# Two-layer diffusion trunk on one core: the first sub-layer's products issued input tile by input tile

## The chip, the cores and the metric

The kernel runs on one core of a Trainium2 chip, as one launch. The metric is device time in microseconds, the median of several runs. TensorE multiplies matrices from SBUF into PSUM, VectorE and ScalarE do element-wise work (VectorE written DVE, ScalarE ACT, TensorE PE in the rows; PEld is TensorE's weight load), GpSimd (POOL) a little, and SyncE (SP) issues nearly all DMAs.

## The reference

Two layers are applied to 128 context tokens and 256 latent tokens with 1024 features. Each layer is: half SwiGLU FFN, token mixing, half SwiGLU FFN, each with an RMS norm and a shift, scale and gate that come from a conditioning vector. The change concerns the input of the very first FFN:

```python
def _modulation(cond, w, b):
    m = jax.nn.silu(cond) @ w + b
    return jnp.split(m[:, None, :], N_MOD, axis=-1)

def _ada_norm(x, g, shift, scale):
    return _rms(x, g) * (1 + scale) + shift

def _half_ffn(x, shift, scale, gate, g, w1, w3, w2):
    h = _ada_norm(x, g, shift, scale)
    f = (jax.nn.silu(h @ w1) * (h @ w3)) @ w2
    return x + 0.5 * gate * f
```

The FFN has 2816 hidden features, 22 tiles of 128. All is fp32; layer 0 mixes tokens by gated linear attention and a Fourier transform, layer 1 by windowed attention.

## The kernel before, in words

Activations lie with features along the partitions: `x` is 8 input tiles of 128 features by 384 tokens. Each fp32 product is made of three float32r matmuls (`mm3`, L336 to L339): high weights by high input, high weights by low input, low weights by high input. A "unit" of weights is 1 MB; for the first FFN a unit holds the 128 columns of w1 and of w3 that make one hidden feature tile. `load_to` (L305) brings units into three raw buffers, `split_to` (L313) makes of each half a high part (ScalarE cast, L210) and a low part (VectorE subtraction, L211), and `take` (L328) hands a unit out after splitting two units and loading four ahead. There are four buffers for high halves and four for low halves, so two units.

The norm's factor 1/rms is applied behind the products: the products' input is `x * (scale + 1) * g`, split into `hh` and `hl` (`Feed.feed`, L225 to L231), and the shift goes along as two more columns, so that a product has 386 columns. `Norm.finish` (L203) makes the mean of the squares by a matmul, then ln and exp on ScalarE and a Newton step of three instructions on VectorE (`rsqrt`, L175 to L185). `combine` (in `ffn`) multiplies a pair of product tiles by 1/rms (L413), applies silu and the product of the two (L418), and splits the result for the second matrix. A pair of product tiles (w1's and w3's columns of one hidden feature tile; "the pair" below) fills a PSUM tile of two banks; the pool `psp` (L53) has three of them.

The first sub-layer's shift and scale are made at the start (L848 to L886), two input tiles at a time, for q = 0 to 3 (the four "groups"): two 1 MB DMAs of modulation weights, 2 x 16 small matmuls into `mod0_q` (L859; a row of the trace counts their 32 parts), a copy, a transposition by TensorE (L868), bias and scale on VectorE, then `shifts` and `feed` for these two input tiles. Everything runs in the order of the built program on each engine; before, a scheduler chose that order on all engines, by priorities that follow the code, and only the products of input tile 4 were told to follow group 3 (`boot`, `behind`). All other modulation vectors come from dot products on VectorE (`mod_dots`, L149) that run beside the FFN, paced by the number of units taken.

Of the kernel before, what the change touches and what calls it, by code (L numbers as in the profile page):

```python
# [17 lines left out]
P = 128  # L18
# [13 lines left out]
MORE = {1: 2, 2: 3}  # attention block behind which a unit of queries is projected  # L32
TURN = {3: 2, 5: 3}  # and is rotated
LAG = 3  # attention blocks between the scores and the products with the values
# (units of weights taken, feature tiles of the modulations done by then)
MOD_PACE = ((2, 0), (34, 42), (38, 42), (45, 48), (50, 48), (112, 120), (123, 120), (150, 128))
PSC = 0.125  # 64 ** -0.5
# [6 lines left out]
def trunk(ctx, tc, a):  # L44
# [19 lines left out]
    # Activations are kept in runs that share a table set, each behind the load of its set.  # L64
# [29 lines left out]
    # the sub-layer's input (T token columns, then the shifts of the two groups), as two float32r parts  # L94
# [16 lines left out]
    # silu(c) as stationary columns: 0 for the context's condition, 1 for the step's.  # L111
# [29 lines left out]
    def mod_dots():  # L141
        """One feature tile of one vector at a time: a dot product along the free axis for either condition."""
# [18 lines left out]
    def pump():  # L161
        """Keeps the modulations as far ahead as the units of weights taken so far ask for."""
        want = np.interp(at["take"], *zip(*MOD_PACE))
        while done[0] < want:
            next(dots)
            done[0] += 1
# [8 lines left out]
    def rsqrt(mean, n, name):  # L175
        """(mean + eps) ** -0.5 by exp and ln, and one Newton step."""
# [10 lines left out]
    class Norm:  # L187
        """RMS statistics of x, built up as its feature tiles become final."""
# [19 lines left out]
    def split(hi, lo, src):  # L208
        """src = hi + lo, both float32r."""
        act.copy(hi, src)  # L210
        pace["last"] = dve.tensor_tensor(lo, src, f(hi), op=ALU.subtract).ins  # L211

    class Feed(Norm):
        """Input of sub-layer n of layer l: x * (scale + 1) * g, and the shift; 1 / rms is applied behind the products."""
# [18 lines left out]
    class Last(Norm):  # L233
        """The final norm, token group by token group."""
# [78 lines left out]
    def split_to(n):  # L313
        while at["split"] < min(n, len(stream)):
# [5 lines left out]
            for h in range(0, w, 1024):  # L320
                e = min(1024, w - h)
                hi = wts.tile([P, e], F32R, tag="whi", name=f"whi{i}_{h}", bufs=4)
                lo = wts.tile([P, e], F32R, tag="wlo", name=f"wlo{i}_{h}", bufs=4)
# [4 lines left out]
    def take(key):  # L328
        i = at["take"]
        assert stream[i][0] == key, (stream[i][0], key)  # L330
        split_to(i + 2)
        load_to(i + 4)
# [9 lines left out]
    def product(out, u, behind=None):  # L342
        """The sub-layer's input @ 128 columns; behind: a feature tile, and an instruction that its products follow."""
        wh, wl = u
        for k in range(KD):
            i = mm3(out, wh[:, k], wl[:, k], hh[:, k], hl[:, k], k == 0, k == KD - 1)
            if behind and behind[0] == k:
                after(i.ins, behind[1], "modulations before the products")

    def spread(dst, pp, feed):  # L350
        """dst [P, 2, T] = products / rms + the shift's products."""
# [6 lines left out]
    def project(key, feed, dst, name):  # L358
        """dst [P, 2, T] = the sub-layer's input @ a unit of 256 columns."""
# [7 lines left out]
    def project_out(nk, parts, l, v, nxt, name, shared=False, order=None):  # L367
        """x += gate * (parts @ w), 256 output features at a time; feeds the next sub-layer as they become final
        (shared: once the last of them has read the parts, which lie where the next input goes)."""
# [36 lines left out]
    def ffn(l, fi, feed, make_next):  # L406
        name = f"ffn{l}{fi}"
        with tc.tile_pool(name=f"g_{name}", bufs=1) as gp:
# [14 lines left out]
            waiting = []  # L423
# [620 lines left out]
```

## Time and profile before

| | |
|---|---|
| timed runs, median (lowest to highest of 3) | 1467.79 us (1466.99 to 1468.07) |
| profiled execution, first to last instruction (span) | 1466.1 us |
| TensorE, matmuls busy | 1429.0 us, 97% |
| TensorE, weight loads busy | 1382.1 us, 94% |
| VectorE busy | 1087.5 us, 74% |
| ScalarE busy | 600.5 us, 41% |
| DMA moved | 245.27 MB, 167 GB/s in the mean |

The profile is of one execution, whose own time on this page is the span; the timed runs hold some 1.7 us more, which lie around it. Busy shares are means over the whole span; busy times by stretch and the sequence of instructions tell where an engine waits. Matmul ends are modelled, so starts are the firmer numbers. The granted TensorE clock is shown as a share of full speed, 1.00 for 2.4 GHz and 0.50 for 1.2 GHz.

### The profile page before, as it was taken

What the parts mean: (1) busy time and instruction counts of PE and PEld (TensorE: products, weight loads), DVE (VectorE), ACT (ScalarE), POOL (GpSimd) and SP (SyncE); (2) the same over time, 40 slices, a digit from 0 to 9 for tenths busy, and PEclk for the clock granted to TensorE, in tenths of its full rate; (3) what the DMA queues carried; (4) which work ended last, traced back from release to release, by engine and by line L of the source; (5) the groups of instructions that cost most, each with busy time, mean ns of one, the idle gap of its engine ahead of it and who ended that gap; (6) DMA issues with size and microseconds to landing.
All of it is one profiled execution on the core that took longest, in us unless ns stands there. A gap on an engine that the chain in (4) does not pass through costs nothing. (4 is left out here: it accounts for less than half of the span.)

```text
span 1466.1 us, 21497 instructions
## 1 busy us (share of the span) xinstructions
PE 1429.0 (97%) x8508; PEld 1382.1 (94%) x8508; DVE 1087.5 (74%) x1825; ACT 600.5 (41%) x976; POOL 98.6 (7%) x74
## 2 busy tenths in 40 slices
PE   6999999999999999999999999999998999999997
PEld 4999999999889999999999999999975999999996
DVE  3799889869876788888869888885577666666433
ACT  3534434335344444343343433333257444434332
POOL 2000000011102000000100000011120200000001
PEclk8999999999999999999999999999999999999998
DMA  9666656563413456556636655654320233433331
GB/s 393 222 208 201 216 193 232 195 226 117 158 44 137 141 197 199 203 176 230 215 141 215 215 187 187 215 219 154 128 87 1 101 125 138 154 130 110 135 101 43
DMA packets 48516, 245.27 MB, mean 167 GB/s; under 512 B 5376, under 2 KB 9856, under 8 KB 29088
## 3 DMA queue, kind: packets, MB, share of 16 engines
q1 hardware_dynamic: 44560, 240.80, 46.9%
q10 hardware_dynamic: 3856, 3.10, 0.7%
q8 instruction: 67, 1.10, 0.3%
q14 instruction: 33, 0.27, 0.1%
HBM read 241.79 MB, written 2.10 MB: 166 GB/s over the span
## 5 line engine op out<-in xcount | busy, mean ns | idle before, releaser
L210 ACT CAST whi<-raw 128x1024 fp32r<-128x1024 f32 (+1 forms) x317 | 325.6, 1028 | 626.9 <-PE ffn_p L338 307.0
L211 DVE TENSOR_TENSOR wlo<-raw,whi 128x1024 fp32r<-128x1024 f32 (+1 forms) x317 | 380.5, 1201 | 191.5 <-ACT whi L210 189.5
L337 PE MATMUL ffn_p<-hh,whi 128*128 128x386 f32 x1408 | 480.0, 341 | 4.9 <-ACT whi L210 3.0
L338 PE MATMUL ffn_p<-hl,whi 128*128 128x386 f32 x1408 | 478.9, 340 | 3.9 <-DVE hl L229 3.7
L339 PE MATMUL ffn_p<-hh,wlo 128*128 128x386 f32 x1408 | 478.9, 340 | 0.3 <-DVE wlo L211 0.2
L149 DVE SCALAR_TENSOR_TENSOR junk<-modw,cb 128x1024 f32<-128x1024 f32 x256 | 314.1, 1227 | 2.1
L338 PEld LDWEIGHTS ffn_p<-hl,whi 128*128 128x128 f32 x1408 | 267.0, 190 | 7.4 <-DVE hl L229 7.0
L337 PEld LDWEIGHTS ffn_p<-hh,whi 128*128 128x128 f32 x1408 | 266.4, 189 | 6.7 <-ACT whi L210 3.2
L339 PEld LDWEIGHTS ffn_p<-hh,wlo 128*128 128x128 f32 x1408 | 266.5, 189 | 1.5 <-DVE wlo L211 1.3
L337 PE MATMUL ffn_acc<-gh_ffn,whi 128*128 128x384 f32 x704 | 236.6, 336 | 0.0
L338 PE MATMUL ffn_acc<-gl_ffn,whi 128*128 128x384 f32 x704 | 236.6, 336 | 0.0
L339 PE MATMUL ffn_acc<-gh_ffn,wlo 128*128 128x384 f32 x704 | 236.6, 336 | 0.0
L337 PEld LDWEIGHTS ffn_acc<-gh_ffn,whi 128*128 128x128 f32 x704 | 132.4, 188 | 0.0
L339 PEld LDWEIGHTS ffn_acc<-gh_ffn,wlo 128*128 128x128 f32 x704 | 132.4, 188 | 0.0
L338 PEld LDWEIGHTS ffn_acc<-gl_ffn,whi 128*128 128x128 f32 x704 | 132.4, 188 | 0.0
L200 POOL TENSOR_TENSOR ssq_n<-ssq_n,sq_n 128x384 f32<-128x384 f32 x42 | 61.0, 1451 | 946.8 <-ACT sq_n L199 922.4
L413 DVE TENSOR_TENSOR ffn_e<-ffn_p,r_n 128x768 f32<-128x768 f32 x88 | 84.0, 955 | 54.2 <-PE ffn_p L339 54.1
L83 ACT ACTIVATE ffn_e<-ffn_e,ffn_wb 128x128 f32<-128x128 f32 (+1 forms) x176 | 70.4, 449 | 53.3 <-DVE ffn_wb L415 53.1
L211 DVE TENSOR_TENSOR gl_ffn<-ffn_e,gh_ffn 128x384 fp32r<-128x384 f32 x88 | 49.0, 557 | 38.1 <-ACT gh_ffn L210 37.9
L210 ACT CAST gh_ffn<-ffn_e 128x384 fp32r<-128x384 f32 x88 | 45.0, 512 | 62.2 <-DVE ffn_e L418 62.2
L418 DVE SCALAR_TENSOR_TENSOR ffn_e<-ffn_e,ffn_p 128x128 f32<-128x128 f32 (+1 forms) x176 | 65.8, 416 | 0.0
L229 DVE SCALAR_TENSOR_TENSOR hl<-x,mods,hh 128x128 fp32r<-128x128 f32 (+1 forms) x96 | 57.1, 636 | 2.0 <-ACT hh L228 1.2
(245 smaller groups left out, 1224.8 us busy)
## 6 DMA issues: line engine op xcount, KB each, us to landing
raw<-in_w SPq DMA_DIRECT2D x120, 1024.0 KB, 4.8
modw<-in_modw SPq DMA_DIRECT2D x128, 512.0 KB, 3.3
raw<-in_w SPq DMA_DIRECT2D x16, 768.0 KB, 4.9
raw_mod<-in_modw SPq DMA_DIRECT2D x8, 1024.0 KB, 15.3
raw<-in_w_in SPq DMA_DIRECT2D x8, 1024.0 KB, 4.8
raw<-in_w_out SPq DMA_DIRECT2D x8, 1024.0 KB, 4.8
raw<-in_w_og SPq DMA_DIRECT2D x2, 1024.0 KB, 5.0
raw<-in_w_v SPq DMA_DIRECT2D x2, 1024.0 KB, 4.7
```

Source lines behind the costliest of these rows:

```text
L83: i = act.activation(out, in_, func, **kw)
L149: i = dve.scalar_tensor_tensor(junk, raw, 1.0, cb[:, c], op0=ALU.mult, op1=ALU.mult, accum_out=mods[l][v][:, d, c : c + 1])
L200: pool.tensor_tensor(self.ssq, self.ssq, sq, op=ALU.add)
L210: act.copy(hi, src)
L211: pace["last"] = dve.tensor_tensor(lo, src, f(hi), op=ALU.subtract).ins
L229: dve.scalar_tensor_tensor(hl[:, d, t0:t1], x[:, d, t0:t1], sc[:, c : c + 1], f(hh[:, d, t0:t1]), op0=ALU.mult, op1=ALU.subtract)
L337: first = pe.matmul(out, lhsT=wh, rhs=mh, start=start, stop=False)
L338: pe.matmul(out, lhsT=wh, rhs=ml, start=False, stop=False)
L339: pe.matmul(out, lhsT=wl, rhs=mh, start=False, stop=stop)
L413: dve.tensor_tensor(e, pp[:, :, :T], feed.r.unsqueeze(1).broadcast_to([P, 2, T]), op=ALU.mult)
L418: dve.scalar_tensor_tensor(e[:, 1, t0:t1], e[:, 1, t0:t1], pp[:, 1, T + c : T + c + 1], e[:, 0, t0:t1], op0=ALU.add, op1=ALU.mult)
```

## The change

The loop over the groups now issues the products of the first three pairs itself, input tile by input tile: after group q's inputs are fed, pair 0 gets its two new input tiles; from q = 1 on also pair 1 (for q = 1 all four input tiles known by then); from q = 2 on also pair 2. On TensorE the order in this part is the order in which the code is written (`manual_schedule`), where a scheduler chose it before. The loads stand in a loop of their own ahead of it: for q = 0 to 2 a unit of weights behind each group's modulation weights, so the third unit now ahead of group 3's; the modulation weights share five buffers where each of the eight had its own. The third unit is split early, into buffers of the start's own pool. Loads of units 3 to 5 now stand ahead of that of the conditions (`cb`). `ffn` finds three pairs begun, finishes the norm first and combines them ahead of the fourth pair. Comments are dropped throughout; the rest of the code is as before.

```diff
-    def split_to(n):
+    def split_to(n, apart=None):
...
-                hi = wts.tile([P, e], F32R, tag="whi", name=f"whi{i}_{h}", bufs=4)
-                lo = wts.tile([P, e], F32R, tag="wlo", name=f"wlo{i}_{h}", bufs=4)
+                if apart is None:
+                    hi = wts.tile([P, e], F32R, tag="whi", name=f"whi{i}_{h}", bufs=4)
+                    lo = wts.tile([P, e], F32R, tag="wlo", name=f"wlo{i}_{h}", bufs=4)
+                else:
+                    hi = apart.tile([P, e], F32R, name=f"whi{i}_{h}")
+                    lo = apart.tile([P, e], F32R, name=f"wlo{i}_{h}")
...
-    def take(key):
+    def take(key, ahead=True):
...
-        split_to(i + 2)
-        load_to(i + 4)
+        if ahead:
+            split_to(i + 2)
+            load_to(i + 4)
...
-    def product(out, u, behind=None):
+    def product(out, u, ks=range(KD)):
         wh, wl = u
-        for k in range(KD):
-            i = mm3(out, wh[:, k], wl[:, k], hh[:, k], hl[:, k], k == 0, k == KD - 1)
-            if behind and behind[0] == k:
-                after(i.ins, behind[1], "modulations before the products")
+        for k in ks:
+            mm3(out, wh[:, k], wl[:, k], hh[:, k], hl[:, k], k == 0, k == KD - 1)
...
-    def ffn(l, fi, feed, make_next):
+    def ffn(l, fi, feed, make_next, begun=()):
...
-            waiting = []
-            for ft in range(NFT):
+            waiting = list(enumerate(begun))
+            if begun:
+                feed.finish()
+            for ft in range(len(begun), NFT):
+                while len(begun) and waiting:
+                    combine(*waiting.pop(0))
                 u = take(("w13", l, fi, ft))
                 pp = two_banks(f"{name}_p{ft}")
                 for i in range(2):
-                    product(pp[:, i, :TX], u[i], boot.get((l, fi, ft, i)))
+                    product(pp[:, i, :TX], u[i])
...
-    feed, boot = Feed(0, 0), {}
-    with tc.tile_pool(name="boot", bufs=1) as bp:
+    feed, begun = Feed(0, 0), []
+    with tc.tile_pool(name="boot", bufs=1) as bp, tc.manual_schedule(engines={mybir.EngineType.PE}):
+        raw_mod = {}
         for q in range(4):
             nc.sync.dma_start(x[:, 2 * q : 2 * q + 2], a["xT"][:, 2 * q : 2 * q + 2])
+            for half in range(2):
+                raw_mod[q, half] = bp.tile([P, 4, 512], F32, tag="raw_mod0", name=f"raw_mod0_{q}{half}", bufs=5)
+                nc.sync.dma_start(raw_mod[q, half], a["modw0"][q, half].rearrange("p (k c) -> p k c", k=4))
+            if q < 3:
+                load_to(q + 1)
+        units = []
+        def begin(ft, ks):
+            if ft == len(begun):
+                units.append(take(("w13", 0, 0, ft), False))
+                begun.append(two_banks(f"ffn00_p{ft}"))
+            for k in ks:
+                for i in range(2):
+                    product(begun[ft][:, i, :TX], units[ft][i], (k,))
+        for q in range(4):
             acc = one_bank(f"mod0_{q}")[:, :P]
             for half in range(2):
-                raw = bp.tile([P, 4, 512], F32, name=f"raw_mod0_{q}{half}")
-                nc.sync.dma_start(raw, a["modw0"][q, half].rearrange("p (k c) -> p k c", k=4))
+                raw = raw_mod[q, half]
...
-                if q == 3:
-                    boot[0, 0, half, 0] = (4, i.ins)
...
             for d in (2 * q, 2 * q + 1):
                 feed.feed(d)
+            if q < 3:
+                split_to(q + 1, bp if q == 2 else None)
             for d in (2 * q, 2 * q + 1):
                 feed.add(d)
-            if q < 2:
-                split_to(q + 1)
-    load_to(3)
+            new = (2 * q, 2 * q + 1)
+            begin(0, new)
+            if q > 0:
+                begin(1, range(4) if q == 1 else new)
+            if q > 1:
+                begin(2, range(6) if q == 2 else new)
+    load_to(6)
...
-    feed = ffn(0, 0, feed, next_feed(0, 1))
+    feed = ffn(0, 0, feed, next_feed(0, 1), begun)
```

TensorE before, from the second pair's products up to group 3 (names: `mod0_2` is group 2's accumulator, `modt0_2` its transposition, `ffn00_p1` the second pair, `whi1` a high part of the second unit; the number at a name's end is a buffer's):

```order
L337 MATMUL ffn00_p1_449<-hh_78,whi1_0_248 128x386
L338 MATMUL ffn00_p1_449<-hl_79,whi1_0_248 128x386
L859 MATMUL mod0_2_257<-raw_mod0_20_258,cs_88 32x128 x16
L339 MATMUL ffn00_p1_449<-hh_78,wlo1_0_249 128x386
L859 MATMUL mod0_2_257<-raw_mod0_21_276,cs_88 32x128 x16
L868 MATMUL modt0_2_296<-ident_75,modrow0_2_294 128x128
L859 MATMUL mod0_3_318<-raw_mod0_30_319,cs_88 32x128 x16
L337 MATMUL ffn00_p0_390<-hh_78,whi0_0_177 128x386
...
L859 MATMUL mod0_3_318<-raw_mod0_31_337,cs_88 32x128 x16
L337 MATMUL ffn00_p1_449<-hh_78,whi1_0_248 128x386
```

TensorE after, at the same groups 2 and 3, with the end of the products ahead of each and the start of those behind it:

```order
L344 MATMUL ffn00_p1_295<-hh_78,wlo1_1024_274 128x386
L883 MATMUL mod0_2_320<-raw_mod0_20_133,cs_88 32x128 x16
L883 MATMUL mod0_2_320<-raw_mod0_21_135,cs_88 32x128 x16
L890 MATMUL modt0_2_355<-ident_75,modrow0_2_353 128x128
L342 MATMUL ffn00_p0_206<-hh_78,whi0_0_194 128x386
...
L344 MATMUL ffn00_p2_408<-hh_78,wlo2_1024_375 128x386
L883 MATMUL mod0_3_445<-raw_mod0_30_140,cs_88 32x128 x16
L883 MATMUL mod0_3_445<-raw_mod0_31_142,cs_88 32x128 x16
L890 MATMUL modt0_3_480<-ident_75,modrow0_3_478 128x128
L205 MATMUL mean_n00_552<-ssq_n00_112,ones_80 128x384
L342 MATMUL ffn00_p0_206<-hh_78,whi0_0_194 128x386
```

Groups 2 and 3 stood within the products that group 1's scale allows, 30 products ahead of group 3's end; now 48 products stand ahead of group 2, 60 more between it and group 3, and 36 behind the mean, before the fourth pair.

ScalarE before, from the last scaled input to the norm's exp (`whi2` is a high part of the third unit, `cb` the conditions, `lnv_n00` the norm's ln, `r0_n00` its exp):

```order
L228 ACTIVATE hh_78<-x_77,mods0_1_93 128x256
L210 CAST whi2_0_439<-raw2_379 128x1024
L83 ACTIVATE cb_110<-cb_110 128x2048
L79 ACT_TABLE_LOAD
L210 CAST whi2_1024_443<-raw2_379 128x1024
L83 ACTIVATE lnv_n00_500<-mean_n00_498,eps_84 128x384
L210 CAST whi3_0_530<-raw3_388 128x1024
L83 ACTIVATE r0_n00_503<-lnv_n00_500 128x384
```

ScalarE after, the third unit's casts at group 2 and then the same place:

```order
L210 CAST hh_78<-mods0_0_92 128x2x2
L210 CAST whi2_0_370<-raw2_137 128x1024
L228 ACTIVATE hh_78<-x_77,mods0_1_93 128x128
...
L228 ACTIVATE hh_78<-x_77,mods0_1_93 128x256
L210 CAST whi3_0_594<-raw3_539 128x1024
L83 ACTIVATE cb_110<-cb_110 128x2048
L79 ACT_TABLE_LOAD
L83 ACTIVATE lnv_n00_554<-mean_n00_552,eps_84 128x384
L210 CAST whi3_1024_598<-raw3_539 128x1024
L83 ACTIVATE r0_n00_557<-lnv_n00_554 128x384
```

The third unit's first cast went ahead of group 2's scaled inputs, the unit that is split at the norm is the fourth, and one cast fewer stands ahead of the ln.

## Rows read from the trace of the kernel before

**Rows 1.** The page: span, busy time by engine, granted clock by slice.

```profile
span 1466.1 us, 21497 instructions
...
PE 1429.0 (97%) x8508; PEld 1382.1 (94%) x8508; DVE 1087.5 (74%) x1825; ACT 600.5 (41%) x976; POOL 98.6 (7%) x74
...
PEclk8999999999999999999999999999999999999998
```

**Rows 2.** Busy time by stretch: start and end, length, then each engine.

```profile
core 0: us, PE busy (x) PEld busy (x) DVE busy (x) ACT busy (x) POOL busy (x), PEclk, DMA share, GB/s
12.50:21.50 9.00, 5.82 (x70) 4.54 (x70) 4.44 (x10) 4.41 (x9) 2.73 (x2) 0.62 1.01 423
21.50:24.90 3.40, 1.54 (x13) 0.80 (x5) 2.25 (x9) 2.08 (x6) 0.00 (x0) 1.00 1.01 417
24.90:28.30 3.40, 3.38 (x11) 2.69 (x10) 2.48 (x3) 2.33 (x4) 1.34 (x1) 0.50 1.02 424
28.30:38.80 10.50, 9.49 (x151) 6.65 (x149) 3.58 (x16) 3.77 (x11) 3.41 (x4) 1.00 1.01 422
75.00:200.00 125.00, 125.00 (x708) 125.00 (x707) 111.45 (x184) 50.93 (x75) 0.00 (x0) 1.00 0.61 207
```

**Rows 3.** The same of the pairs' products alone (PE, PEld, DVE, clock).

```profile
12.50:38.80 26.30, 11.62 (x36) 7.77 (x36) 0.00 (x0) 0.81 1.01 422
38.80:57.95 19.15, 19.14 (x107) 18.92 (x108) 3.36 (x8) 1.00 0.68 254
57.95:66.47 8.52, 8.52 (x50) 8.52 (x49) 1.77 (x4) 1.00 0.36 123
```

**Rows 4.** TensorE in order of time: start, duration, instruction, idle before.

```profile
15.43 0.69 PE L337 MATMUL ffn_p<-hh,whi 128*128 128x386 f32 x1 [2.97 <-ACT whi L210]
...
17.50 0.52 PE L338 MATMUL ffn_p<-hl,whi 128*128 128x386 f32 x1
17.82 0.53 PE L339 MATMUL ffn_p<-hh,wlo 128*128 128x386 f32 x1
18.28 3.48 PE L859 MATMUL mod<-raw_mod,cs 128*32 128x128 f32 x64
...
23.86 0.44 PE L337 MATMUL ffn_p<-hh,whi 128*128 128x386 f32 x1 [1.35 <-ACT hh L228]
...
27.88 0.53 PE L339 MATMUL ffn_p<-hh,wlo 128*128 128x386 f32 x1
...
30.60 1.08 PE L859 MATMUL mod<-raw_mod,cs 128*32 128x128 f32 x32
...
37.19 0.27 PE L868 MATMUL modt<-ident,modrow 128*128 128x128 f32 x1
...
38.81 0.62 PE L337 MATMUL ffn_p<-hh,whi 128*128 128x386 f32 x2 [0.19 <-ACT hh L228]
```

**Rows 5.** ScalarE in order of time, from the third unit's cast to the exp.

```profile
40.69 1.05 ACT L210 CAST whi<-raw 128x1024 fp32r<-128x1024 f32 x1 [1.24 <-PE ffn_p L338]
41.64 1.92 ACT L83 ACTIVATE cb<-cb 128x2048 f32<-128x2048 f32 x1
43.57 1.28 ACT L79 ACT_TABLE_LOAD   x1
...
45.90 0.58 ACT L83 ACTIVATE lnv_n<-mean_n,eps 128x384 f32<-128x384 f32 x1
...
47.31 0.53 ACT L83 ACTIVATE r_n<-lnv_n 128x384 f32<-128x384 f32 x1
```

**Rows 6.** VectorE in order of time.

```profile
15.41 2.36 DVE L211 TENSOR_TENSOR wlo<-raw,whi 128x1024 fp32r<-128x1024 f32 x2 [0.45 <-ACT whi L210]
...
33.36 1.58 DVE L229 SCALAR_TENSOR_TENSOR hl<-x,mods,hh 128x128 fp32r<-128x128 f32 x4 [0.31 <-ACT hh L228]
...
53.74 0.74 DVE L418 SCALAR_TENSOR_TENSOR ffn_e<-ffn_e,ffn_p 128x128 f32<-128x128 f32 x2
```

**Rows 7.** The longest wait of TensorE from 38 to 1440 us (total, times, longest).

```profile
PE sc L786 <- ACT pw L83: 1.2, 1, 1.2
```

More of the change, by code (lines that the diff above doesn't have):

```diff
@@ L846, in mixer_swa @@
         return nxt
-    feed, boot = Feed(0, 0), {}
-    with tc.tile_pool(name="boot", bufs=1) as bp:
+    feed, begun = Feed(0, 0), []
+    with tc.tile_pool(name="boot", bufs=1) as bp, tc.manual_schedule(engines={mybir.EngineType.PE}):
+        raw_mod = {}
         for q in range(4):
             nc.sync.dma_start(x[:, 2 * q : 2 * q + 2], a["xT"][:, 2 * q : 2 * q + 2])
+            for half in range(2):
[12 more added lines that the diff above has]
+        for q in range(4):
             acc = one_bank(f"mod0_{q}")[:, :P]
             for half in range(2):
-                raw = bp.tile([P, 4, 512], F32, name=f"raw_mod0_{q}{half}")
-                nc.sync.dma_start(raw, a["modw0"][q, half].rearrange("p (k c) -> p k c", k=4))
+                raw = raw_mod[q, half]
                 for k in range(4):
                     for j in range(4):
-                        i = pe.matmul(
+                        pe.matmul(
                             acc[32 * j : 32 * j + 32, :], lhsT=cs[:, 4 * half + k, :], rhs=raw[:, k, j * P : j * P + P],
```

## Prediction, on record before the result

> **What bounds the kernel now.** I read the page's shares first: TensorE is busy 97% of a span of 1466.1 us, and the clock line is low in the first and the last slice only [rows 1]. So the next view is busy time by stretches. From 75 to 200 us TensorE is busy 125.00 of 125.00 us, while VectorE has 111.45 [rows 2], and between 38 and 1440 us its longest single wait is 1.2 us [rows 7]. Whatever moves the moment at which TensorE becomes dense moves the end by the same amount. That moment is 38.8 us. Ahead of it, from 12.5 us on, TensorE has only 36 of the first products, at a mean clock of 0.81; then the 108 that are left of the first three pairs follow in 19.15 us, 0.177 us each, and the fourth pair starts at 57.95 us [rows 3]. The last view is the sequence of instructions on TensorE, ScalarE and VectorE up to there [rows 4 to 6]. The fourth pair needs a PSUM tile: there are three, and the first pair's is free when VectorE has read it for the last time, at 53.74 + 0.74 = 54.48 us [rows 6]. So before, the norm's chain (mean, ln, exp, three Newton steps, first combination) ends 3.5 us before TensorE wants its result, and is hidden.
>
> The span's 1466.1 us is 1.7 us below the median of the timed runs, 1467.79; I add differences in the trace to the median.
>
> **The change part by part.** The arithmetic is the same: 144 products for three pairs, eight groups of 32 modulation matmuls, the same splits. What changes is the sequence on TensorE. Before, the second, third and fourth groups of modulation matmuls stand among or ahead of products, and 36 products are ahead of the last scale. After, 12 products precede group 1, 36 more precede group 2, 60 more precede group 3: 108 in all. I follow the clock through the new sequence.
>
> *Up to group 1.* Until the first product at 15.43 us nothing moves. The low part of the first unit's second half is done at 15.41 + 2.36 = 17.77 us [rows 6]. Before, only products with the first half stood there, and group 1 started at 18.28. Now all 12 stand there, 7 of them not before that second low part; at 17.82 - 17.50 = 0.32 us each [rows 4] they end at 20.1. Group 1 took 3.48 us, mostly at half clock; the clock rises near 21.5 [rows 2], so 1.4 us do 40% of it, and the rest takes 60% of 2.16 (two halves at 1.08 [rows 4]): it ends at 22.8 us, against 21.76 before.
>
> *Up to group 2.* From the end of group 1 to the first product with its scale went 23.86 - 21.76 = 2.1 us [rows 4]; so 24.9. Twelve products then took 4.35 us (23.86 to 27.88 is eleven of them) at half clock [rows 2, 4]: 29.3. The 24 of the second pair at 0.177: 33.5 us. Group 2's data is long there (before, its second half ran at 30.60). It ends at 33.5 + 2.16 = 35.7.
>
> *Up to group 3.* Again 2.1 us, but ScalarE now has the third unit's first cast, 1.05 us [rows 5], between the shift's cast and the scaled inputs, and VectorE that unit's low part, 2.36 / 2 = 1.18 us [rows 6], ahead of the inputs' low parts: first product at 38.8. The first pair's 12 are paced by the low parts (1.58 us for a pair of tiles [rows 6]), some 2.6 us; the other 48 take 8.5: 49.9 us. TensorE has then idled nearly 3 us, and the trace shows what follows such a gap: after 2.97 us [rows 4] the granted clock was down, 0.62 in the mean of 12.5 to 21.5 [rows 2], which is half from about the restart to 21.5; after 1.35 us it was 0.50 until 28.3. So 4.4 to 6 us at half clock, which lose 2.2 to 3.0; zero if the clock holds. I take 2.5: 52.4 us. Group 3, whose data (before, in place by 36) comes 2.5 us later because 1 MB for the third unit is now queued ahead of it (420 GB/s [rows 2]), waits for nothing: 54.6, its transposition at 55.1 us. Before, that was at 37.19.
>
> *The tail.* From that transposition to the first pair's free PSUM tile went 54.48 - 37.19 = 17.3 us. The chain keeps its order: ScalarE first waits for a weight buffer that the first pair's last products release (cast at 40.69), then silu of the conditions 1.92, a table load 1.28, ln, exp [rows 5]. One cast of 1.05 us moves from ahead of ln to behind it: 16.3 us, with 17.3 as the other end if VectorE, which still has two low parts ahead of the Newton steps, gives nothing back. So the fourth pair may start at 71.3 us.
>
> What covers the chain is the point of the change's cost. Before, 108 products lay behind the last scale, 19 us of work. Now 36 do: they start 38.81 - 37.19 = 1.6 us behind the transposition and last 6.4, so TensorE is through by some 63.5 us and waits 7.8 us for PSUM. What is queued behind that waiting product is the whole rest of the kernel.
>
> *The clock after the wait.* The fourth pair comes back after an idle stretch longer than either in the rows. At half clock for 4.4 to 6 us after the restart it loses 2.2 to 3.0 us. The rows at the other side are the later waits of up to 1.2 us [rows 7], after which the clock line stays at 9 [rows 1]: zero. The gap is nearest to the long one, but part of the low stretch passes while TensorE still waits; I take 2.2. The Trainium skill speaks against the change here: its page "TensorE: Matmul & The Clock Gate", section "HAM oscillation — how this bites in real kernels", says that a TensorE that waits between bursts comes back throttled and pays half of that time, and describes the same for waits on PSUM. By that rule the sum keeps this term, +15.6 us; by the short waits it would be +13.4. The two gaps at the start agree with the rule.
>
> *The rest.* The six raw buffers' loads and the conditions' load are issued later by SyncE (the load of unit 5 needs unit 2's raw buffer, split at about 41.5, and the conditions stand behind it), but ScalarE reaches that silu only near 60: hidden; if not, it would lengthen the chain one for one. The products of units 3 and 4 find their weights split during the wait. VectorE has two combinations more to catch up than before at the fourth pair; its slack is 13.55 us in 125 [rows 2], and three pairs' results may wait in PSUM, so I cost that at nothing, and at half a pair's products, 24 at 0.177 or 4.3 us, if it does not fit.
>
> **Sum.** 71.3 + 2.2 - 57.95 = +15.6 us: span 1481.7, median 1483.4 us. The ends: no half clock at either place and the 12 products of the second step at full clock too give +9; 3.0 us lost at both, the second pair's products slow as well (+2) and no microsecond saved in the tail, +20.
>
> **The rivals.** *TensorE is not held.* If the modulation groups were taken up as their data lands, while products wait, the last transposition would come at most by the 2.5 us of the third unit later than before: 37.19 + 2.5 = 39.7; + 16.3 + 2.2 = 58.2 us against 57.95, so 1468.0, no change; with the half-clock term gone too, 1465.8, faster by 0.1%, and with the data no later than before 1463.3, by 0.3%. The break-even is a last transposition at 39.4 us. For it speaks that the data is there and that TensorE's time before 38.8 is only partly used. Against it: in the rows TensorE's instructions start in the order of the program, and group 2 ran before only when the products ahead of it had been issued. The Trainium skill's page "PSUM — Partial Sum Buffer", section "Engine vs sequencer instructions", says that matmuls start and complete in program order; by that rule this rival is out.
>
> *The clock holds.* Same chain, but no half clock behind either gap: +15.6 - 2.5 - 2.2 = +10.9, 1478.7 us. For it: the waits after 38.8 never lowered it. Against it: two gaps of 1.35 and 2.97 us did.
>
> *VectorE becomes the bound.* The combinations that pile up behind the chain delay the split weights of the following pairs: +4.3, 1487.7 us. For it: 89% busy. Against it: the next units are split during TensorE's wait.
>
> *The order is not what bounds*: the fourth pair starts as its products reach TensorE, without the chain; 63.5 - 57.95 gives +5.6, 1473.4 us. It would take a fourth PSUM tile, which the pool does not have.
>
> **How the numbers follow.** My forecast, +13 to +18: 66%. The clock holds: 16%. VectorE: 8%. Without the chain: 4%. Not held: 6%, split between no change and faster. Predicted 1483 us; range 1475 to 1488, which leaves out the two last and what goes over +20. This measurement tells about 0.2% from no change, 2.9 us: faster 3%, same 5%, slower 92%.
>
> **What would show it.** In the changed profile: group 2 starts near 33.5 and group 3 near 52 us; the ln of the first norm near 64; one TensorE wait of 6 to 9 us for the first combination, ahead of the fourth pair, near 71; a clock below full near 39 to 45 and again behind the wait; from there on the same dense work, shifted by one constant. I am wrong if group 3 starts before 42 us, if no such wait stands in front of the fourth pair, or if the distance to before changes much after 100 us.

## The result and the profile after

| | before | after |
|---|---|---|
| timed runs, median (lowest to highest; count) | 1467.93 us (1466.99 to 1468.38; 4) | 1481.98 us (1480.55 to 1482.76; 4) |
| ratio after / before, 95% interval | | 1.0096 [1.0084, 1.0108] |
| span of the profiled execution | 1466.1 us | 1478.8 us |
| start of the fourth pair on TensorE | 58.20 us | 68.89 us |

The kernel became 14 us slower; 1483.0 had been forecast, with 1475 to 1488 as its range. The profiled execution is the quickest of the four after.

The start of the fourth pair before is 58.20 us, not the 57.95 that the prediction takes from [rows 3]: the three pairs have 144 products, and counted in order of time the last of them starts at 58.02 us. The next row is

```profile
58.20 0.34 PE L337 MATMUL ffn_p<-hh,whi 128*128 128x386 f32 x1
```

The page of the changed kernel, against [rows 1]: TensorE's busy time hardly differs (1430.5 us, before 1429.0), and the span is 12.7 us longer. The time is idle time in the first slices.

```profile
span 1478.8 us, 21498 instructions
...
PE 1430.5 (97%) x8508; PEld 1384.2 (94%) x8508; DVE 1087.1 (74%) x1825; ACT 600.0 (41%) x976; POOL 98.0 (7%) x74
...
PEclk9899999999999999999999999999999999999999
```

Busy time of the pairs' products alone, by stretch (start and end, length, TensorE, granted clock, DMA), against [rows 2, 3]. From 38.80 to 57.95 us, where before TensorE was full with 19.14 us of products, it has 15.09; in the next 8.52 us, where before the fourth pair's 48 products ran almost from the start, it has 3.54. Behind 75 us it is as full as before (125.00 of 125.00 us up to 200).

```profile
24.90:28.30 3.40, 3.31 (x17) 1.00 0.99 413
28.30:38.80 10.50, 4.64 (x22) 0.98 1.02 422
38.80:57.95 19.15, 15.09 (x77) 0.92 0.50 200
57.95:66.47 8.52, 3.54 (x20) 0.95 0.21 63
```

TensorE in order of time (start, duration, instruction, idle before it and what ended it), against [rows 4]. The groups of modulation matmuls are the `mod` rows, at 20.13, 32.28 and 50.45 us; the last row is the fourth pair's first product. Group 3's transposition, at 37.19 us before, stands at 52.82.

```profile
20.13 2.45 PE L883 MATMUL mod<-raw_mod,cs 128*32 128x128 f32 x64
...
24.69 0.44 PE L342 MATMUL ffn_p<-hh,whi 128*128 128x386 f32 x1 [1.35 <-ACT hh L228]
...
32.28 1.96 PE L883 MATMUL mod<-raw_mod,cs 128*32 128x128 f32 x64
...
37.11 0.44 PE L342 MATMUL ffn_p<-hh,whi 128*128 128x386 f32 x1 [2.13 <-ACT hh L228]
...
50.45 1.95 PE L883 MATMUL mod<-raw_mod,cs 128*32 128x128 f32 x64
52.82 0.33 PE L890 MATMUL modt<-ident,modrow 128*128 128x128 f32 x1 [0.41 <-DVE modrow L888]
52.98 0.82 PE L205 MATMUL mean_n<-ssq_n,ones 128*128 128x384 f32 x2
54.50 0.44 PE L342 MATMUL ffn_p<-hh,whi 128*128 128x386 f32 x1 [0.69 <-ACT hh L228]
...
68.89 0.66 PE L342 MATMUL ffn_p<-hh,whi 128*128 128x386 f32 x1 [7.41 <-DVE ffn_wb L418]
```

The chain that ends those 7.41 us, on ScalarE, against [rows 5]: a weight cast that waits for the first pair's last products, silu of the conditions, a table load, ln, exp.

```profile
56.56 1.05 ACT L210 CAST whi<-raw 128x1024 fp32r<-128x1024 f32 x1 [1.42 <-PE ffn_p L343]
57.51 1.91 ACT L83 ACTIVATE cb<-cb 128x2048 f32<-128x2048 f32 x1
59.43 1.28 ACT L79 ACT_TABLE_LOAD   x1
60.73 0.58 ACT L83 ACTIVATE lnv_n<-mean_n,eps 128x384 f32<-128x384 f32 x1
...
62.14 0.52 ACT L83 ACTIVATE r_n<-lnv_n 128x384 f32<-128x384 f32 x1
```

And on VectorE, against [rows 6]: Newton steps, a low part, the first pair's combination. Its last read of the PSUM tile is the L421 row, which ends at 68.75; 0.14 us later TensorE goes on.

```profile
63.41 0.55 DVE L182 SCALAR_TENSOR_TENSOR u_n<-mean_n,r_n 128x384 f32<-128x384 f32 x1
...
65.07 1.22 DVE L211 TENSOR_TENSOR wlo<-raw,whi 128x1024 fp32r<-128x1024 f32 x1
66.20 0.95 DVE L416 TENSOR_TENSOR ffn_e<-ffn_p,r_n 128x768 f32<-128x768 f32 x1
...
68.00 0.75 DVE L421 SCALAR_TENSOR_TENSOR ffn_e<-ffn_e,ffn_p 128x128 f32<-128x128 f32 x2
```

The granted clock is half from 65.5 to 72.4 us, so the first 3.5 us of the fourth pair run at half speed and lose 1.75. 68.89 + 1.75 - 58.20 = 12.4 us, and the span grew by 12.7: the start explains all but 0.3. The same distance stands in the rest: ln of the second norm is 12.38 us later than before (338.77 against 326.39), of the third 12.34 (492.03 against 479.69), of the sixth 12.37 (1203.72 against 1191.35). The 0.3 us that are missing come behind the sixth norm's ln.

### The profile page after: what moved, and what is told of

Read it like the earlier page. It is cut to its first block, busy times and chain, and to the rows that moved or that the text cites. A ratio compares the mean times of both kernels' runs of the same rounds, so it can differ in the third digit from the quotient of the medians.

```text
span 1478.8 us, 21498 instructions
## 1 busy us (share of the span) xinstructions
PE 1430.5 (97%) x8508; PEld 1384.2 (94%) x8508; DVE 1087.1 (74%) x1825; ACT 600.0 (41%) x976; POOL 98.0 (7%) x74
## 5 line engine op out<-in xcount | busy, mean ns | idle before, releaser
L421 DVE SCALAR_TENSOR_TENSOR ffn_e<-ffn_e,ffn_p 128x128 f32<-128x128 f32 (+1 forms) x176 | 66.1, 417 | 0.9 <-ACT ffn_e L83 0.8
```

The source lines that it names most:

```text
L421: dve.scalar_tensor_tensor(e[:, 1, t0:t1], e[:, 1, t0:t1], pp[:, 1, T + c : T + c + 1], e[:, 0, t0:t1], op0=ALU.add, op1=ALU.mult)
```

## The experiments

Nine kernels ran. Each ratio is to executions of the kernel before that were timed beside that run (medians 1467.56 to 1468.26 us). "Start" is the fourth pair's first product in the profiled execution, 58.20 us before; where no wait stands in front of it, it is the 145th product in order of time; "second ln" is the start of the second norm's ln there, against before's 326.39 us, and tells what the start was worth ahead of the token mixer. All but the first two columns are of the profiled execution, which need not be the median one.

| run | median us (lowest to highest; count) | ratio to before [95%] | start us | second ln us | granted clock at half, near |
|---|---|---|---|---|---|
| not pinned | 1480.77 (1480.24 to 1481.94; 4) | 1.0091 [1.0075, 1.0108] | 68.88 | +12.04 | 38-41, 65-72 |
| group 3 early | 1478.28 (1477.45 to 1479.58; 4) | 1.0069 [1.0054, 1.0084] | 66.02 | +9.86 | 36-43, 64-70, 477-480 |
| norm early | 1477.63 (1474.60 to 1480.58; 4) | 1.0057 [1.0037, 1.0077] | 64.39, no wait | +6.19 | 37-44, 57-61, 395-409 |
| norm ahead of silu | 1479.22 (1478.80 to 1479.43; 4) | 1.0074 [1.0059, 1.0089] | 61.80, no wait | +4.38 | 15-21, 25-28, 38-42, 393-407 |
| the same, 7 us added | 1479.76 (1479.43 to 1481.02; 4) | 1.0084 [1.0069, 1.0099] | 69.12, no wait | +11.24 | 37-44, 478-481 |
| wait filled | 1482.47 (1479.91 to 1486.08; 4) | 1.0102 [1.0081, 1.0123] | 68.63 | +10.51 | 38-41, 400-413 |
| both groups early | 1466.66 (1465.83 to 1469.14; 10) | 0.9991 [0.9981, 1.0000] | 55.78 | -2.3 | none |
| mended | 1468.39 (1464.87 to 1471.20; 10) | 1.0001 [0.9992, 1.0010] | 57.44, no wait | -0.75 | 15-22, 26-29, 466-469 |
| mended, copy first | 1472.39 (1464.04 to 1472.91; 12) | 1.0016 [1.0002, 1.0030] | 56.59, no wait | -1.59 | 15-22, 26-29, 388-401 |

(Half clock in the last 12 us of every run, in which TensorE has nothing to do, is left out. Before has it near 15-21 and 25-28, the changed kernel near 14-21, 38-42 and 65-72.)

The second ln follows the start: start less 58.20, plus what half clock behind the start costs, gives it within 0.4 us, but for the norm ahead of silu (4.4 against 3.6), where a wait of 0.51 us stands inside the fourth pair.

### Is it the pinning, or the order as written?

```diff
-    with tc.tile_pool(name="boot", bufs=1) as bp, tc.manual_schedule(engines={mybir.EngineType.PE}):
+    with tc.tile_pool(name="boot", bufs=1) as bp:
```

> The changed kernel's code with the scheduler free to choose TensorE's order in the start, as it was before the change. Theory A (the cost lies in the order in which the code is written, with 108 products ahead of the last scale; the pinning only fixes what the priorities would give as well): the same long chain, one cast of 1 us more ahead of ln: 1481 to 1484 us, and a PSUM wait of 7 to 9 us ahead of the fourth pair. Theory B (the pinning is what costs; a free scheduler moves the modulation groups ahead of the products): group 3 before 42 us, 1466 to 1470 us.

TensorE of that run: group 3 one microsecond earlier than in the changed kernel, the same 68.88 us for the fourth pair.

```profile
49.48 1.96 PE L883 MATMUL mod<-raw_mod,cs 128*32 128x128 f32 x64
...
68.88 0.66 PE L342 MATMUL ffn_p<-hh,whi 128*128 128x386 f32 x1 [8.73 <-DVE ffn_wb L418]
```

1480.77 us, below the 1481 to 1484 that theory A had by a quarter of a microsecond, far from B's 1466 to 1470. The pinning is not the cost: the priorities follow the code and leave groups 2 and 3 behind 48 and 108 products; the pairs' products between the groups come partly in another order. TensorE is through the three pairs 1.3 us earlier (8.73 us of wait against 7.41, at the same start), and it gains nothing: the fourth pair's start is set by the chain. The cost lies in where the code puts the products.

### Group 3 earlier, and nothing else

```diff
-            begin(0, new)
-            if q > 0:
-                begin(1, range(4) if q == 1 else new)
-            if q > 1:
-                begin(2, range(6) if q == 2 else new)
+        group(2)
+        begin(0, (4, 5))
+        begin(1, (4, 5))
+        group(3)
+        begin(2, (0, 1))
+        begin(0, (6, 7))
+        begin(1, (6, 7))
+        begin(2, range(2, 8))
```

> The changed kernel with group 3's modulation matmuls ahead of the third pair's products (36 products earlier), and the last input tiles' products of pairs 1 and 2 ahead of most of pair 3's. The norm's mean then comes behind all products of the three pairs. Theory A: group 3 starts near 43.5 us instead of 50.45 and TensorE is through the three pairs near 59, but the chain begins only there (mean 0.8, ln 0.6, exp 0.5, Newton 1.7, first combination about 3.6 with its silu): the fourth pair starts near 66.5, after a wait of about 7 us; 1479.5 us. Rival B: bringing the last group 7 us forward gives 7 us back, 1475 us.

TensorE of that run. The mean of the squares is at 59.53 us although the last transposition is at 46.65: it is written behind all products, in `ffn`.

```profile
44.28 1.95 PE L883 MATMUL mod<-raw_mod,cs 128*32 128x128 f32 x64
46.65 0.33 PE L890 MATMUL modt<-ident,modrow 128*128 128x128 f32 x1 [0.41 <-DVE modrow L888]
...
59.53 0.81 PE L205 MATMUL mean_n<-ssq_n,ones 128*128 128x384 f32 x2
...
66.02 0.66 PE L342 MATMUL ffn_p<-hh,whi 128*128 128x386 f32 x1 [5.68 <-DVE ffn_wb L418]
```

Group 3 came 6.2 us earlier and the fourth pair 2.9; 1478.28 us is nearer to theory A's 1479.5 than to B's 1475. So it isn't group 3 as such on which the fourth pair waits, but the norm's chain.

### The norm earlier

With the mean, and the last squares with it, ahead of the third pair's products:

```diff
+            if q == 2:
+                for d in (6, 7):
+                    feed.add(d)
+                feed.finish()
...
-            if begun:
-                feed.finish()
```

> The changed kernel with the norm's mean put on TensorE ahead of the third pair's first products (behind the 24 products of group 2's tiles), and the squares of the last two input tiles ahead of it; the groups of modulation matmuls and the products stay in the changed kernel's sequence. Theory A (the fourth pair waits for the first pair's PSUM tile, which the norm's chain frees, and only 36 products cover that chain): the fourth pair starts when TensorE is through the third, at about 61.5 us instead of 68.9, with no wait above 1 us ahead of it and no half clock behind it; 1482.0 - 7.4 - 1.7 = 1472.9 us. Rival B (the cost is that groups 2 and 3 come late, and the PSUM wait only stands where another would): group 3 still starts near 50.4, the wait turns into one for the fourth unit's weights, 1480 to 1482 us.

And with the mean where the change has it, but ScalarE's silu of the conditions written behind the norm:

```diff
             if begun:
                 feed.finish()
+                actf(cb, cb, AF.Silu, "silu")
...
-    actf(cb, cb, AF.Silu, "silu")
```

> The changed kernel with the conditions' silu written behind the norm instead of ahead of it, which lets ScalarE take the norm's ln directly behind the last scaled inputs, ahead of the cast that waits for a weight buffer; TensorE's sequence is that of the changed kernel. Theory A: ln near 55 us instead of 60.7, the first pair's PSUM tile free near 61 to 62 instead of 68.9; the fourth unit's casts come later and may cost up to 1 us; 1472.5 to 1474.5 us. Rival B: TensorE's sequence, which makes the groups late, is unchanged, so 1480 to 1482 us.

In both the 7.41 us wait for PSUM is gone, with group 3 as late as in the changed kernel (51.97 and 50.94 us). With the norm ahead of silu the fourth pair follows the third without a gap, and one short wait for a low part stands inside it:

```profile
61.80 0.34 PE L342 MATMUL ffn_p<-hh,whi 128*128 128x386 f32 x1
...
62.82 0.44 PE L344 MATMUL ffn_p<-hh,wlo 128*128 128x386 f32 x1 [0.51 <-DVE wlo L211]
```

The second norm's ln is 6.2 and 8.0 us earlier than in the changed kernel: that is what the chain had cost at the start. The 1.8 between the two is mostly half clock from 57 to 61 us in the first, which lay over back-to-back products, 1.4 us behind a wait of 1.35 us, and cost 1.7. Theory A's cause came in both (no wait for PSUM), its time in neither: it had 1472.9 and 1472.5 to 1474.5, and only 4.4 and 2.8 us reached the medians. With the norm early, two of the four executions took 1474.6 and 1475.0 us, 7.2 under the changed kernel, and two 1480.2 and 1480.6; the profiled one is of the latter. Where the rest went in the profiled executions is the token mixer, between the second and the third norm's ln. Busy time there, by stretch, in the kernel before:

```profile
326.39:389.00 62.61, 62.05 (x383) 57.85 (x383) 56.39 (x90) 32.52 (x49) 9.73 (x8) 1.00 0.43 151
389.00:402.60 13.60, 13.60 (x111) 10.99 (x110) 9.49 (x25) 1.66 (x5) 2.54 (x2) 1.00 0.18 63
402.60:479.69 77.09, 75.32 (x482) 70.77 (x481) 50.64 (x85) 33.97 (x60) 11.78 (x8) 1.00 0.26 90
```

and with the norm ahead of silu:

```profile
330.77:393.40 62.63, 62.07 (x384) 57.87 (x385) 56.44 (x90) 32.50 (x49) 9.75 (x8) 1.00 0.43 151
393.40:407.10 13.70, 13.70 (x70) 8.86 (x69) 7.64 (x20) 0.58 (x1) 2.53 (x2) 0.50 0.07 24
407.10:490.25 83.15, 81.37 (x523) 76.63 (x522) 52.48 (x91) 35.06 (x62) 11.77 (x8) 1.00 0.26 89
```

The columns are TensorE, its weight loads, VectorE, ScalarE, GpSimd, then the granted clock. The first stretch takes the same time in both. In the second, TensorE is busy throughout in both, with the mixer's small matmuls; at clock 1.00 it does 111 recorded groups in 13.60 us, at 0.50 only 70 in 13.70. What it did not do is in the third stretch, 83.15 instead of 77.09 us: 6.2 us in all. The changed kernel has 1.00 there:

```profile
401.40:415.00 13.60, 13.60 (x111) 10.98 (x110) 9.48 (x25) 1.67 (x5) 2.53 (x2) 1.00 0.17 63
```

### Is the half clock behind the wait due to the wait?

Eleven matmuls whose result nobody reads are added behind the third pair's last product:

```diff
             if begun:
                 feed.finish()
+                warm = one_bank("warm")[:, :T]
+                for n in range(11):
+                    pe.matmul(warm, lhsT=ones, rhs=f(hh[:, KD - 1, :T]), start=(n == 0), stop=(n == 10))
```

> The changed kernel with eleven more matmuls of 0.64 us each, whose result nobody reads, behind the third pair's last product: TensorE works through the 7.4 us in which it waited for PSUM. Theory A (the clock falls after the wait because TensorE stood still): no half clock from 65 us on, the fourth pair still starts at 68.9 us, and the 1.65 us that its slow products cost come back: 1480.3 us. Theory B (the low clock there does not come from the wait): 1482 us, the half clock stays. If the added work itself were on the path, 1489 us.

TensorE of that run (a row counts two parts of each added matmul), and its busy time by stretch from 60 us on:

```profile
61.03 7.26 PE L431 MATMUL warm<-hh,ones 128*128 128x384 f32 x22
...
68.63 0.42 PE L342 MATMUL ffn_p<-hh,whi 128*128 128x386 f32 x1 [0.34 <-DVE ffn_wb L418]
```

```profile
60.00:68.00 8.00, 8.00 (x29) 5.00 (x27) 5.92 (x9) 6.46 (x9) 0.00 (x0) 1.00 0.39 131
68.00:75.00 7.00, 6.66 (x37) 6.40 (x37) 5.65 (x13) 3.89 (x8) 0.00 (x0) 1.00 0.41 151
```

The changed kernel's, in the same stretches:

```profile
60.00:68.00 8.00, 1.49 (x9) 1.17 (x7) 5.66 (x8) 6.67 (x9) 0.00 (x0) 0.85 0.37 131
68.00:75.00 7.00, 6.11 (x25) 6.14 (x26) 5.53 (x14) 3.25 (x9) 0.00 (x0) 0.68 0.40 151
```

The clock is 1.00 in both stretches (0.85 and 0.68 in the changed kernel), the fourth pair starts 0.26 us earlier and the second ln 1.87: the 0.26 and 1.6 of the half clock. Theory A holds, at the start, and the other profiles agree: the three with a wait of 5.7 to 8.7 us ahead of the fourth pair (changed, not pinned, group 3 early) have half clock there, the eight whose wait is under 1 us have none from 62 to 75 us. The median doesn't show it: two executions took 1479.9 and 1480.0 us, 2.0 under the changed kernel, and two 1485.0 and 1486.1; the profiled one is of the latter, and its mixer is at half clock from 400 to 413 us.

### Does the half clock in the mixer belong to the early norm?

The kernel with the norm ahead of silu, with the same eleven unread matmuls behind the third pair's last product (the three lines above):

> The run with the norm ahead of silu of the conditions, and the same eleven unread matmuls behind the third pair's last product: 7.0 us of work added on the path. It shifts everything behind by about 7 us, to where the changed kernel has it. Theory A (the half clock in the token mixer, near 393 to 407 us in that run, depends on when TensorE arrives there, not on what it did in the first 70 us): the mixer runs at full clock again, 1479.2 + 7.0 - 6.2 = 1480.0 us. Theory B (it comes with the early norm as such): 1486.2 us, and the half clock is there again, some 7 us later.

```profile
62.32 7.26 PE L432 MATMUL warm<-hh,ones 128*128 128x384 f32 x22
```

```profile
400.20:413.90 13.70, 13.70 (x111) 11.09 (x112) 9.54 (x25) 1.73 (x5) 2.54 (x2) 1.00 0.19 65
```

7.26 us of work on the path cost 0.5 us in the median (1479.22 to 1479.76). In the profiled executions the second norm's ln comes 6.9 us later and the third's 2.2: this stretch of the mixer ran at full clock again, which gave 6.2 back, and 3.4 us of half clock at 478 us took 1.5. So the early norm as such isn't the cause, and 1480.0 was theory A's number. But A's reason, the time at which TensorE arrives, is not shown: by the second norm's ln, the clock fell in this stretch of the profiled executions with +4.4, +6.2 and +10.5 us and -1.6, and held at 0, -2.3, -0.7, +9.9, +11.2, +12.0 and +12.4; and one and the same kernel with the norm early has two executions near 1480.4 us and two near 1474.8. What decides it stays open.

### A version that should beat both

Groups 2 and 3 ahead of the second and third pairs' products, and the norm between:

```diff
+        group(2)
+        squares(2)
+        begin(1, range(4))
+        squares(3)
+        begin(0, (4, 5))
+        begin(1, (4, 5))
+        feed.finish()
+        group(3)
+        begin(2, range(6))
+        begin(0, (6, 7))
+        begin(1, (6, 7))
+        begin(2, (6, 7))
```

> The pinned sequence with group 2 ahead of the second pair's 24 products, group 3 ahead of the third pair's 36, and the norm's mean ahead of group 3. Theory A: TensorE finds work behind each transposition, so the waits of 2.1 and 0.8 us in front of group 2's inputs go, with the half clock there, and the fourth pair starts when TensorE is through, near 53 us against 57.95 in the kernel before: 1463 us (1461 to 1465). Rival C (the weights bound it: the fourth unit is split only when the first pair's last products release its buffers, near 49 us, so its second half is late): fourth pair near 53 but waits of 2 to 4 us inside it, 1466 to 1467 us.

```profile
26.63 2.10 PE L881 MATMUL mod<-raw_mod,cs 128*32 128x128 f32 x64
...
38.56 1.96 PE L881 MATMUL mod<-raw_mod,cs 128*32 128x128 f32 x64
41.83 0.33 PE L888 MATMUL modt<-ident,modrow 128*128 128x128 f32 x1 [1.32 <-DVE modrow L886]
...
55.78 0.42 PE L342 MATMUL ffn_p<-hh,whi 128*128 128x386 f32 x1 [0.89 <-DVE ffn_e L421]
```

The fourth pair starts 2.4 us earlier than before, the second ln 2.3, and the span is 2.1 us shorter (1464.0). Part of that is the clock: this execution has none of the half clock that before's has near 15 to 21 and 25 to 28 us. It isn't the 53 us expected: VectorE had the copy of group 3's result behind three Newton steps (1.32 us), and the first pair's PSUM tile came 0.89 late. The median is 15.3 us under the changed kernel's and level with before (1466.66 us; theory A had 1463, rival C 1466 to 1467, but no wait for weights stands in the fourth pair's way). The loads in their new order, the shared modulation buffers and the third unit's own buffers are all still in this kernel, so none of them is what the change cost. Two mends of these places followed:

```diff
+            if q == 3:
+                begin(2, range(4))
...
+        feed.finish(lambda: group(3))
+        begin(0, (6, 7))
+        begin(1, (6, 7))
+        begin(2, range(4, 8))
```

> Groups 2 and 3 early as in the run with both, and three places of it mended: the copy of group 3's result is not behind the last two Newton steps (1.3 us of wait there), 24 products of the third pair cover the way from group 3's transposition to its scaled inputs, and the first pair's last products come ahead of the third pair's last 24, so that the weight and PSUM buffers come free earlier. Theory A (the start of the fourth pair sets the time, one for one): fourth pair near 53.5 us, against 55.8 there and 57.95 before; 1464.4 us, 0.15 to 0.3 per cent under before. Theory B (something behind the start, VectorE catching up, gives it back): 1466 to 1468 us.

Here the scheduler left the copy where it was (the same 1.32 us), and only the 0.89 went. The fourth pair starts at 57.44 us, not 53.5, in an execution with the same two half-clock stretches at the start as before's; the median is 1468.39, above both theories, the fastest of ten 1464.87. In the next run a dependency put the copy ahead of the second Newton step:

```diff
-        dve.scalar_tensor_tensor(u, u, -0.5, r0, op0=ALU.mult, op1=ALU.mult)
+        i = dve.scalar_tensor_tensor(u, u, -0.5, r0, op0=ALU.mult, op1=ALU.mult)
+        if first:
+            after(i.ins, first, "inputs before the norm")
```

> The mended version, with the copy of group 3's result now ahead of the second Newton step on VectorE, which the scheduler had not done in the run before. Theory A (the start of the fourth pair sets the time, and the clock's half stretches in the start and in the mixer come on top of it): no wait of 1.3 us for that copy, fourth pair 12.2 us behind the mean of the norm (17.0 to 17.9 in the two runs with both groups early), so near 54.5 us in an execution without half clock ahead of it and near 57 with two such stretches; 1463.5 to 1465 us and 1466.5 to 1468 us in the two cases, median near 1466, 0.1 per cent under before. Theory B (VectorE behind the start gives it back): the second norm's ln comes no earlier than in the run with both, 1466.7 us or more in the fastest execution.

```profile
40.61 0.81 PE L208 MATMUL mean_n<-ssq_n,ones 128*128 128x384 f32 x2
41.35 1.95 PE L884 MATMUL mod<-raw_mod,cs 128*32 128x128 f32 x64
43.72 0.33 PE L891 MATMUL modt<-ident,modrow 128*128 128x128 f32 x1 [0.41 <-DVE modrow L889]
```

The wait is 0.41 us, and from there to the fourth pair no wait is left. My 12.2 us from the mean to the fourth pair was a slip: 3.1 us to the transposition and 72 products at 0.177 make 15.9, and the fourth pair starts at 56.59 us in this execution, which had half clock near 15 to 22 and 26 to 29 us (A had some 57 for that case). Theory B's sign, a second ln no earlier than in the run with both, came too (-1.59 against -2.3 us), but that run had full clock at its start. The fastest two of 12 executions took 1464.04 and 1464.33, inside theory A's 1463.5 to 1465 and below B's 1466.7; neither was profiled. The profiled one lost 6 us in the mixer as above,

```profile
386.90:400.60 13.70, 13.70 (x75) 8.74 (x74) 7.69 (x22) 0.59 (x1) 2.53 (x2) 0.52 0.11 39
400.60:484.29 83.69, 81.90 (x524) 77.15 (x524) 52.98 (x91) 35.05 (x63) 11.80 (x8) 1.00 0.26 89
```

and eight of the 12 lie, like it, between 1472.2 and 1472.9. The median is 4.4 us over before, where A had 1466. No version beat before beyond what this can measure: with the same half clock at the start the fourth pair comes 1.6 us earlier than before, and half clock in the mixer, which none of these edits touches, takes 6.2 in many executions. The kernel before may have it at times: 2 of 47 executions of it took 1473 us, 5 over its median; they were not profiled.

## Why the prediction was right

The forecast was of the right sign, size and mechanism; its three clock terms were each too high, by 3 us together (1.8, 0.8 and 0.45), and waits that it had left out gave some 0.8 of that back.

*Program order holds TensorE.* Group 2 stood behind 48 products and started at 32.28 us (33.5 forecast), group 3 behind 108 and started at 50.45 (52.4). The rival "not held" is refuted by those two rows and by the run with both groups early, where the same data is multiplied at 26.63 and 38.56 us: it was there and TensorE did not take it up.

*Up to group 2*, 1.2 us too late in the forecast. Group 1 ended at 22.58 (22.8) and the first product with its scale came at 24.69 (24.9), but I let the next 12 products run at half clock, because the kernel before did after the same 1.35 us gap. After the change the clock held there (1.00 from 24.90 to 28.30): these 12 took 2.56 us, not 4.35, and the 24 behind them 5.03, not 4.2, with a wait for a low part among them. Among before, after and the nine runs, five profiles have half clock near 14 to 22 us and four of these also near 25 to 29. It doesn't go by the order: the norm ahead of silu has the changed kernel's order and gap up to there, and its clock fell near 25 us. One profile of before could not tell.

*Up to group 3*, 0.7 us more. The first product with group 2's scale came at 37.11 us, behind a wait of 2.13 where I had put nearly 3; a second wait, of 0.78 for a low part, ended at 38.33. The clock did fall, from 38.2 to 41.7 us: the products ran 3.4 us of it at half speed and lost 1.7, not 2.5. Group 3 with its transposition took 2.37 us, not 2.7.

*The tail* was right: 52.82 to 68.89 is 16.07 us, 16.3 forecast and 17.3 as its other end. The saved cast is visible: the second cast of the unit split at the norm stands behind ln (at 61.20), where before it stood ahead of it. The chain is in the order forecast, and the wait for the first combination is 7.41 us, 7.8 forecast. (TensorE was through the three pairs at 61.5 us; the forecast's 63.5 should have been 63.1 by its own terms, 55.1 + 1.6 + 6.4.)

*The clock after the wait* cost 1.75 us, not 2.2: it fell at 65.5, while TensorE still waited, and only 3.5 us of the low stretch lay over products. The rival "the clock holds" had neither term; the clock fell at both places, and the filled wait shows that at the second one the wait was the reason. At the first, nothing was filled, and the reason is not shown. The Trainium skill's page "TensorE: Matmul & The Clock Gate", section "HAM oscillation — how this bites in real kernels", says that a TensorE that waits between bursts restarts throttled; with 1.9 us gained by filling the wait, the runs agree here.

*VectorE* did not become the bound: it does 112.76 us of work from 75 to 200 us, 1.3 more than before, while TensorE is full, and the distance to before stays at 12.34 to 12.38 us from the second norm to the last.

```profile
75.00:200.00 125.00, 125.00 (x707) 125.00 (x707) 112.76 (x186) 49.70 (x74) 0.00 (x0) 1.00 0.59 200
```

*Without the chain* would have been +5.6 us. The norm ahead of silu is that case: group 3 late, no wait ahead of the fourth pair, its start 3.6 us later than before and the second ln 4.4. So of the 12.4 us that the changed kernel lost at the start, about 4.4 are the late groups and TensorE's waits among them, and about 8 the norm's chain with no products left to cover it, the clock behind the wait included. I had split it 5.6 and 10.

*The sum*: the fourth pair started 2.4 us earlier than forecast (2.3 of it from the transposition), the clock after the wait cost 0.45 less, and the start before was read 0.25 too early: 15.6 less these is 12.5, against 12.4 at the second ln and 12.7 in the span. The median grew by 14.05 all the same, since the profiled execution is 1.4 us under it; the closeness to 1483.0 is partly luck.

## What to carry to other kernels

Where an engine takes its work in program order, as TensorE did here, work that is ready early is not free filling: what is put ahead of the last link of a dependent chain can delay the chain, and what is taken from behind it uncovers the chain's end. Count what stands behind the last input of the longest chain (here 36 products, 6.4 us, against 16.1 us of chain), and issue the chain's own short instructions first. Time from one profile that depends on the granted clock belongs in the range, not in the sum.

## What the runs showed that was not expected

The clock can fall in a stretch in which the records show TensorE always busy. In the token mixer, amid small matmuls (outputs of 64 x 128 to 128 x 256), it went to half for 13.7 us and cost 6.2 us in four of the eleven profiled executions, each time 62 to 63 us behind the second norm's ln. In three others (group 3 early, 7 us added, mended) it went to half for 3.4 us, 11 to 15 us ahead of the third norm's ln, and cost 1.5. The profiled times, and it seems the medians, moved with it: a saving of 8.0 us at the start was worth 2.8 in the end, and 7.26 us of added work cost 0.5. Why it falls in one execution and not in the next is open.
